# The end of the output projection, the second norm and the first MLP products under a list scheduler

## The chip, the cores and the metric

The kernel runs on one NeuronCore of a Trainium2 chip. Its engines work in parallel, each through its own queue in order: TensorE (PE; PEld is its weight load), VectorE (DVE), ScalarE (ACT), GpSimd (POOL) and SyncE (SP), which issues most DMA transfers. The metric is device time in microseconds (us), the median of several runs. A profiled execution is one run of its own, and times inside it are counted from the start of its span.

## The reference

One layer of an encoder: 1024 tokens, model width 1024.

```
h = rmsnorm(x, norm_mix_w);  proj = h @ w_in        # z, xBC, dt, q, k, v
y_ssm = ssd_mixer(...)                              # (1024, 1024)
y_na  = neighbourhood_attention(q, k, v, ...)       # 16 heads of 64
x = x + concatenate([y_ssm, y_na], axis=-1) @ w_out # w_out: 2048 x 1024
h = rmsnorm(x, norm_mlp_w)
out = x + square(relu(h @ w_mlp_in)) @ w_mlp_out    # d_ff = 4096
```

All of it is float32. The kernel splits each factor into a high part (float32r) and a low part, the rest, and forms each product from three matmuls: high by high, high by low, low by high (`mm3`, L361, and `chain`, L1217).

## The kernel before

Four phases follow each other: projection and scan; attention with the first three quarters of the w_out product beside it; the last quarter, the second norm and the first MLP product; the second MLP product.

**The planner.** The work of the scan and of the attention phase is not emitted in program order. It is entered as tasks in a `Plan` (L85), each with its engine, a cost in us, the buffers it reads and writes, and a due time for some. `order` (L141) carries due times back from each task to those it depends on. Then it takes, again and again, the task that could start first by the costs (rounded to 0.35 us), and among equals the one with the earlier due. `ready` (L182) gives the start: engine free, inputs done plus a margin (0.9 us for PE, 0.25 for the others), and a buffer of the ring free; `rings` says how many there are of each kind. `follow` (L135) takes over the free times of the plan before, and buffers entered as given count as ready at once. `run` (L1203) emits the tasks in that order and pins it on each engine (`in_order`, L1186). Instructions outside a plan are ordered by the framework (L1912 opens it with `schedule_with_timeline_sim=True`); it may move them ahead of others on their engine.

**Attention (L1249 to L1512).** Heads are worked in eight pairs. `attend` (L1351) computes scores on PE, shifts and exponents on DVE and ACT, transposes and splits the weights, and multiplies by v on PE. The result of a pair is copied from PSUM into a tile yT by ACT (L1388) and completed by DVE (L1389). `divide` (L1457) divides it on POOL (L1478), with the denominators turned and spread through DRAM on SP, and pair by pair it is stored to `na_dr` on SP ("nast"). The ring of yT holds two tiles. The planner's due for the store is 36 us after the pair's last scores.

**Last quarter of w_out (L1588 to L1607).** w_out has 2048 rows; a quarter is 512 rows. The quarters 0 to 2 are tasks of the attention plan. The weights of the last one for output columns 0 to 511 are loaded and split in that plan as well (`out_weights`, L490; L1511), without a due time; they use the ring of three split weights that the third quarter's also use. Then, outside any plan, the loop over the eight token tiles runs: for each of two column halves four steps of three matmuls into a PSUM tile "po" from a ring "mm" of two banks; an add to x2 on DVE (L1597); the store of the sum to `x2_dr` (L1598); its square sum on ACT (L1601), the root on POOL (L390, L391), the scaling on DVE in place (L1603).

**Factors and first products (L1565 to L1630, L1737 to L1749).** The MLP products use Strassen's scheme: seven products of half matrices. The left factors are seven sums and differences of quarters of the normalized x2, turned: `factors` (L1572) turns factors 1, 2 and 3 and forms the differences in place on DVE (L1585), `t_factor` (L1625) turns 6, 5, 7 and 4. Each of the 28 turned groups is four PE transposes into a PSUM tile (rings "tp" and "s", two banks each), a copy on ACT (L372) and a subtraction on DVE (L373). Products 1 and 2 of weight block 0 and product 1 of block 1 are placed among them (L1737 to L1749). Two of the three use split weights in side tiles that lie in the space of factor 4.

**The rest.** The loop over eight weight blocks (L1753) issues the other products, and the last phase the second MLP product.

Of the kernel before, what the change touches and what calls it, by code (L numbers as in the profile page):

```python
# [10 lines left out]
F32 = mybir.dt.float32  # L11
F32R = mybir.dt.float32r
# [218 lines left out]
def hymba_block(  # L231
# [258 lines left out]
    def out_weights(plan, part_, h, k2, due=None):  # L490

        Buf, task = plan.buf, plan.task
        raw, w = Buf("raw"), Buf("w")
        r0 = 512 * part_ + 256 * k2

        def load():
            raw.t = wp.tile([P, 1024], F32, tag="wraw", name="wraw", bufs=2)
            nc.sync.dma_start(
                raw.t.rearrange("p (a f) -> p a f", a=2),
                w_out[0][r0 : r0 + 256, 512 * h : 512 * h + 512].rearrange("(a p) f -> p a f", p=P),  # L500
            )

        def high():
            w.t = [wp.tile([P, 1024], F32R, tag=t, name=t, bufs=3) for t in ("wh", "wl")]
            nc.scalar.activation(w.t[0], raw.t, AF.Copy)

        def low():
            nc.gpsimd.tensor_tensor(w.t[1], raw.t, w.t[0].bitcast(F32), op=sub)
# [733 lines left out]
    with ExitStack() as ph:  # L1242
# [21 lines left out]
        for pool_, tag, n, shape, d in (  # L1264
            (cb, "nam", 1, [P, 7 * P], F32),
            (cb, "braw", 1, [P, 384], F32),
            (cb, "mb", 2, [P, 7 * P], F32),
            (ap, "pth", 1, [P, NT, 3, P], F32R),
            (ap, "ptl", 1, [P, NT, 3, P], F32R),
            (ap, "nmx", 2, [P, 8], F32),  # L1270
            (ap, "pr", 4, [P, 384], F32),
            (ap, "den", 2, [P, 2, 8], F32),
            (yt, "yT", 2, [P, T], F32),
            (ap, "rd", 1, [16, P], F32),
            (ap, "rb", 1, [P, T], F32),
        ):
            make[tag] = partial(pool_.tile, shape, d, tag=tag, name=tag, bufs=n)
# [179 lines left out]
        def divide(p, yT, yparts, den, at):  # L1457
# [43 lines left out]
        for p in range(8):  # L1501
# [13 lines left out]
        def get0(k):  # L1515
            hi, lo = get0_w[k // 2].t
            s = slice((k % 2) * 512, (k % 2) * 512 + 512)
            return hi[:, s], lo[:, s]
# [10 lines left out]
        wq, hA = (  # L1529
            b0s.enter_context(tc.tile_pool(name=n, bufs=1, side="right", reuse_waits="tile"))  # L1530
            for n in ("wq", "hA")
        )
        hc = {}

        def hc_tile(i, n):
            if i in (5, 6):
                tag = {(6, 0): "q", (6, 1): "k", (5, 0): "v", (5, 1): "kl"}[i, n]
                return b0.tile([P, 4, 512], F32R, tag=tag, name=f"h{i}", bufs=1)
            return hA.tile([P, 4, 512], F32R, tag=f"h{i}{n}", name=f"h{i}")

        def side_pair(i, n):
            t = hA.tile([P, 2, 1024], F32R, tag=f"h{i}{n}", name="wside")
            return t[:, 0], t[:, 1]

        for i in (1, 2, 3):
            hc[i] = [hc_tile(i, n) for n in range(2)]
        np_ = ph.enter_context(tc.tile_pool(name="np", bufs=2, reuse_waits="tile"))
        wb = np_.tile([P, D], F32, name="wb2", bufs=1)
        nc.sync.dma_start(wb, norm_mlp_w.partition_broadcast(P)[:, 0, :])
        h1 = []  # L1550
        for k2 in range(2):
            raw = wp.tile([P, 1024], F32, tag="wraw", name="wraw", bufs=2)
            r0 = 1536 + 256 * k2
            nc.sync.dma_start(
                raw.rearrange("p (a f) -> p a f", a=2),
                w_out[0][r0 : r0 + 256, 512:1024].rearrange("(a p) f -> p a f", p=P),
            )
            h1.append(side_pair(7, k2))
            split_to(h1[k2], raw, (nc.gpsimd, nc.vector)[k2])

        def get1(k):
            s = slice((k % 2) * 512, (k % 2) * 512 + 512)
            return h1[k // 2][0][:, s], h1[k // 2][1][:, s]

        def turned(src, i, t, tag):  # L1565
            pt = tag("ptn")
            for j in range(4):
                nc.tensor.transpose(pt[:, j * P : (j + 1) * P], src[:, j * P : (j + 1) * P], ident)
            s = (slice(None), slice(None), slice(t * P, t * P + P))
            split_from_psum(hc[i][0][s], hc[i][1][s], pt.rearrange("p (j t) -> p j t", j=4))  # L1570

        def factors(t):  # L1572
            if t < 4:
                turned(x2[:, t, 0:512], 1, t, ps_tp)
                turned(x2[:, t, 512:1024], 2, t, ps_s)
                return
            u, v = x2[:, t - 4, :], x2[:, t, :]
            turned(v[:, 512:1024], 3, t - 4, ps_tp)
            for o, p, q in (
                (u[:, 0:512], v[:, 0:512], u[:, 0:512]),  # L1580
                (v[:, 0:512], v[:, 512:1024], v[:, 0:512]),
                (v[:, 512:1024], v[:, 512:1024], u[:, 0:512]),
                (u[:, 512:1024], u[:, 512:1024], v[:, 512:1024]),
            ):
                nc.vector.tensor_tensor(o, p, q, op=sub)  # L1585

        before = None
        for t in range(NT):  # L1588
            xt = x2[:, t, :]
            for h, get in enumerate((get0, get1)):  # L1590
                pt = ps_mm("po")
                s = slice(t * P, (t + 1) * P)
                for k in range(4):
                    yh, yl = last[k]
                    mm3(pt, yh[:, s], yl[:, s], *get(k), k == 0, k == 3)
                d = xt[:, h * 512 : (h + 1) * 512]
                nc.vector.tensor_tensor(d, d, pt, op=add)  # L1597
            nc.sync.dma_start(x2_dr[t], xt)  # L1598
            jk = np_.tile([P, D], BF16, tag="jk", name="jk", bufs=1)
            ss = np_.tile([P, 1], F32, tag="ss", name="ss")  # L1600
            nc.scalar.activation(jk, xt, AF.Square, accum_out=ss)  # L1601
            r = inv_rms(np_, ss, D, 1, "r0")
            nc.vector.scalar_tensor_tensor(xt, xt, r, wb, op0=mul, op1=mul)  # L1603
            if before is not None:
                factors(before)
            before = t

    raws, hls = [wp] * 2 + [wq] * 6, [wp] * 3

# [8 lines left out]
    with ExitStack() as ph:  # L1618
# [3 lines left out]
        phase["mm"] = 4  # L1622
        hq = None

        def t_factor(i):  # L1625
            hc[i] = [hc_tile(i, n) for n in range(2)]
            for t in range(4):
                u, v = x2[:, t, :], x2[:, t + 4, :]
                src = {6: v[:, 512:1024], 5: u[:, 0:512], 7: v[:, 0:512], 4: u[:, 512:1024]}[i]
                turned(src, i, t, ps_s)  # L1630

        class Block:


            def __init__(self, fb):
                self.fb = fb
                self.a = {}
                self.load("11")
                self.X = [ps_mm("px1") for _ in range(2)]
                self.w = {}  # L1640

            def load(self, *names):
                for n in names:
# [272 lines left out]
```

## Time and profile before

| | |
|---|---|
| median of 3 runs | 1607.6 us (1606.81 to 1608.2) |
| the profiled execution | 1602.66 us |
| its span | 1600.9 us, 20796 instructions |
| DVE, ACT, POOL busy | 63%, 45%, 45% of the span |
| granted TensorE clock, mean | 0.992 |
| DMA | 278.73 MB, mean 174 GB/s |

Busy columns name the share of time in which an engine had work; PEclk is the clock granted to TensorE, as a share of its full speed. A busy TensorE at a lower clock does less. A row of waits names who waited for whom, the sum in us, how often and the longest. In the timeline a row has start, duration, engine, line, operation, output and input, and in brackets the idle time before it with what ended it. Matmuls are pipelined, and their ends are modelled: they overlap the next start.

### The profile page before, as it was taken

How to read it: one execution, taken by the hardware profiler on the slowest of the kernel's cores; microseconds unless marked ns; L12 is line 12 of the kernel's file. 1: busy time of each engine (PE TensorE's matmuls, PEld its weight loads, DVE VectorE, ACT ScalarE, POOL GpSimd, SP SyncE). 2: the span in 40 equal slices, each digit the busy share in tenths (PEclk: the TensorE clock that was granted, in tenths of full speed). 3: DMA queues.
4: the chain of work that ended last, by engine and by line, in shares of the span. 5: the costliest groups of instructions: out<-in, count | busy, mean ns of one | idle time of the engine just before them, and what ended most of it. 6: DMA issues, size and time to landing. Idle time of an engine off the chain costs nothing. (4 is left out here: it accounts for less than half of the span.)

```text
span 1600.9 us, 20796 instructions
## 1 busy us (share of the span) xinstructions
PE 1560.6 (97%) x7462; PEld 1290.7 (81%) x7462; DVE 1016.3 (63%) x1420; ACT 722.1 (45%) x1187; POOL 717.1 (45%) x524
## 2 busy tenths in 40 slices
PE   7999999999999999999999998999999989999999
PEld 5788888888878888888888776888888777888887
DVE  3776454787688845667776574544444488877763
ACT  5444333444344435657676234544444434333330
POOL 2000066774789823242364331444444465565551
PEclk9999999999999999999999999999999989999999
DMA  8212497777778786988773411444443685444232
GB/s 222 55 40 69 98 315 262 221 237 252 221 218 226 223 251 178 248 228 237 196 200 119 145 66 53 171 145 151 152 145 140 223 305 196 174 158 144 94 105 79
DMA packets 184226, 278.73 MB, mean 174 GB/s; under 512 B 14819, under 2 KB 106043, under 8 KB 184123
## 3 DMA queue, kind: packets, MB, share of 16 engines
q1 hardware_dynamic: 133323, 233.88, 48.3%
q10 hardware_dynamic: 49792, 39.85, 7.6%
q0 software_dynamic: 1008, 3.67, 0.6%
q8 instruction: 59, 0.97, 0.2%
q14 instruction: 44, 0.36, 0.1%
HBM read 191.51 MB, written 89.18 MB: 175 GB/s over the span
## 5 line engine op out<-in xcount | busy, mean ns | idle before, releaser
L368 POOL TENSOR_TENSOR wl<-wraw,wh 128x1024 fp32r<-128x1024 f32 x114 | 309.5, 2726 | 331.2 <-ACT wh L367 320.6
L367 ACT ACTIVATE wh<-wraw 128x1024 fp32r<-128x1024 f32 x126 | 132.2, 1054 | 174.7 <-PE px L1219 51.6
L362 PE MATMUL pq<-wh,hTh 128*128 128x512 f32 x512 | 204.6, 400 | 2.2 <-DVE qn L929 1.7
L363 PE MATMUL pq<-wl,hTh 128*128 128x512 f32 x512 | 200.1, 391 | 0.2 <-DVE wl L882 0.2
L364 PE MATMUL pq<-wh,hTl 128*128 128x512 f32 x512 | 200.1, 391 | 0.0
L1219 PE MATMUL px<-wh,ahl 128*128 128x512 f32 x512 | 162.6, 395 | 3.3 <-ACT ahl L367 3.3
L1219 PE MATMUL px<-h,wh 128*128 128x512 f32 x496 | 155.7, 394 | 1.4 <-DVE x L1597 1.4
L368 DVE TENSOR_TENSOR ahl<-ar,ahl 128x1024 fp32r<-128x1024 f32 x56 | 115.3, 2065 | 25.3 <-ACT ahl L367 24.2
L367 ACT ACTIVATE ahl<-ar 128x1024 fp32r<-128x1024 f32 x56 | 58.3, 1051 | 141.5 <-PE px L1219 75.0
L1219 PEld LDWEIGHTS px<-wh,ahl 128*128 128x128 f32 x512 | 97.2, 190 | 25.0 <-ACT ahl L367 3.7
L362 PEld LDWEIGHTS pq<-wh,hTh 128*128 128x128 f32 x512 | 96.3, 188 | 22.2 <-DVE qn L929 2.1
L364 PEld LDWEIGHTS pq<-wh,hTl 128*128 128x128 f32 x512 | 96.1, 188 | 20.6
L1219 PEld LDWEIGHTS px<-h,wh 128*128 128x128 f32 x496 | 92.7, 187 | 24.5 <-ACT h L372 1.6
L363 PEld LDWEIGHTS pq<-wl,hTh 128*128 128x128 f32 x512 | 96.3, 188 | 19.4 <-DVE wl L882 0.7
L1219 PE MATMUL px<-wl,ahl 128*128 128x512 f32 x256 | 101.1, 395 | 0.0
L1219 PE MATMUL px<-h,wl 128*128 128x512 f32 x248 | 97.7, 394 | 0.0
L1335 POOL TENSOR_TENSOR mb<-braw,nam 128x256 f32<-128x256 f32 (+1 forms) x48 | 38.6, 831 | 106.0 <-DVE nmx L1404 81.8
L1416 ACT ACTIVATE pr<-pr,nmx 128x384 f32<-128x384 f32 (+1 forms) x128 | 74.6, 584 | 19.6 <-DVE nmx L1404 19.0
L1219 PE MATMUL pz<-h,wh 128*128 128x512 f32 x256 | 81.7, 399 | 0.8 <-DVE h L373 0.8
L1438 DVE TENSOR_TENSOR ptl<-ptp,pth 128x384 fp32r<-128x384 f32 (+1 forms) x128 | 65.5, 521 | 26.0 <-ACT pth L1440 24.9
L1219 PE MATMUL pz<-wh,ahl 128*128 128x512 f32 x256 | 80.7, 391 | 0.8 <-DVE ahl L368 0.8
L362 PE MATMUL po<-wh,yh 128*128 128x512 f32 x192 | 80.6, 420 | 0.0
(324 smaller groups left out, 3777.5 us busy)
## 6 DMA issues: line engine op xcount, KB each, us to landing
ar<-act_dr SPq DMA_DIRECT2D x56, 512.0 KB, 3.9
act_dr<-cq SPq DMA_DIRECT2D x49, 512.0 KB, 3.2
wraw<-in_w_in_dram SPq DMA_DIRECT2D x44, 512.0 KB, 7.3
rb<-cum_dr SPq DMA_DIRECT2D x32, 512.0 KB, 6.5
wraw<-in_w_mlp_in_dram SPq DMA_DIRECT2D x32, 512.0 KB, 4.9
wraw<-in_w_mlp_out_dram SPq DMA_DIRECT2D x32, 512.0 KB, 4.7
q_dr<-hl ACTq DMA_DIRECT2D x16, 512.0 KB, 5.0
k_dr<-hl ACTq DMA_DIRECT2D x16, 512.0 KB, 3.6
```

Of the source, the lines that this page charges most:

```text
L362: nc.tensor.matmul(pt, lhsT=ah, rhs=bh, start=first, stop=False)
L363: nc.tensor.matmul(pt, lhsT=ah, rhs=bl, start=False, stop=False)
L364: return nc.tensor.matmul(pt, lhsT=al, rhs=bh, start=False, stop=last)
L367: nc.scalar.activation(hl[0], src, AF.Copy)
L368: eng.tensor_tensor(hl[1], src, hl[0].bitcast(F32), op=sub)
L1219: nc.tensor.matmul(pt, lhsT=a, rhs=b, start=f, stop=l, skip_group_check=True)
L1335: nc.gpsimd.tensor_tensor(mb.t[:, s].rearrange("p (s r c) -> p s r c", r=16, c=8), view()[:, a:b], nam.t[:, s].rearrange("p (s r c) -> p s ...
L1416: nc.scalar.activation(pr.t[:, 0:n], pr.t[:, 0:n], AF.Exp, bias=nmx.t[:, b : b + 1], scale=-1.0, accum_out=den.t[:, hh, b : b + 1],)
L1438: nc.vector.tensor_tensor(lo[0], pv3, hi.bitcast(F32), op=sub)
```

## The change

Three things change.

The ring of yT gets a third tile, and the due time of the store to `na_dr` moves from 36 to 24 us.

The weights of the last quarter for the first column half get due times (280 and 281).

The code outside the plans from L1514 to L1607 and L1737 to L1749 is replaced by a third plan. Its PSUM ring "mm" has four banks. The sixteen po groups run in a new order of token tiles; the first three are all of the first column half. Tiles 5, 6 and 7 are normalized into buffers "xn" of their own, the others in place. The four differences per pair of tiles stay; for the first three pairs two of them go to POOL. The split weights of the three first products use the ring of three, and no side tiles in the space of factor 4; the side tiles of the second half's weights (in the space of factor 7) stay. Products and transposes have due times, in us from the start of the plan. The rest of the kernel is untouched.

```diff
-            | {"nmx": 2, "pr": 4, "den": 2, "yT": 2, "rd": 1, "rb": 1}
+            | {"nmx": 2, "pr": 4, "den": 2, "yT": 3, "rd": 1, "rb": 1}
...
-            (yt, "yT", 2, [P, T], F32),
+            (yt, "yT", 3, [P, T], F32),
...
-                sp(512, lambda: na_dr[p], lambda: yT.t, reads=[yT], writes=[NA[p]], name="nast", due=at + 36)
+                sp(512, lambda: na_dr[p], lambda: yT.t, reads=[yT], writes=[NA[p]], name="nast", due=at + 24)
...
-        get0_w = [out_weights(plan, 3, 0, k2) for k2 in range(2)]
+        get0_w = [out_weights(plan, 3, 0, k2, 280.0 + k2) for k2 in range(2)]
...
-        k0 = Block(0)
-        k0.split(1)
-        k0.split(2, side_pair(4, 0))
-        k0.product(1)
-        factors(7)
-        k0.load("12", "21", "22")
-        t_factor(6)
-        k0.product(2)
-        k1 = Block(1)
-        k1.split(1, side_pair(4, 1))
-        t_factor(5)
-        t_factor(7)
-        k1.product(1)
-        t_factor(4)
+        before = plan
+        plan = Plan(
+            {"mm": 4, "tp": 2, "s": 2, "w": 3, "raw": 2, "wq": 6, "jk": 1, "ss": 2, "r0": 2, "xn": 3}
+            | {f"h{i}{n}": 1 for i in (1, 2, 3, 4, 7) for n in range(2)}
+            | {t: 1 for t in ("q0", "k0", "v0", "kl0")}
+        )
...
+        Y3 = [plan.given(Buf(tag)) for tag in ("q0", "k0", "v0", "kl0")]
+        w0 = [plan.given(Buf("w"), b.t) for b in get0_w]
...
+        XB = [Buf("xn") if t > 4 else None for t in range(NT)]
...
+        def block_product(kb, i, raw, tag, due):
+            w = split_task(raw, Buf("w"), "POOL")
...
+                    task("PE", 0.682, products, reads=[w, H[i, 0], H[i, 1]], writes=[pt], due=due + 2.75 * j + 0.69 * k, name=f"k{kb.fb}{i}")
...
+        def turned(x, h, i, t, tag, due):
...
+            task("PE", 0.44, turn, reads=[XN[x][h]], writes=[pt], due=due, name="ptn")
+            task("ACT", 0.69, lambda: nc.scalar.activation(H[i, 0].t[s], view(), AF.Copy), reads=[pt], writes=[HP[i, 0, t]], name="hi")
...
+        groups = [(0, 0), (1, 0), (2, 0), (0, 1), (1, 1), (2, 1), (4, 0), (4, 1)]
+        groups += [(3, 0), (3, 1), (5, 0), (5, 1), (6, 0), (6, 1), (7, 0), (7, 1)]
+        for m, (t, h) in enumerate(groups):
+            pt, d, at = Buf("mm"), x2[:, t, halves_[h]], 3.2 * m
...
+                task("PE", 0.682, products, reads=[Y3[k], (w0, w1)[h][k // 2]], writes=[pt], due=at + 0.7 * k, name="po")
...
+            load(512, partial(lambda t: x2_dr[t], t), partial(lambda xt: xt, xt), reads=X2[t], due=at + 12, name="x2st")
...
+            if t < 4:
+                turned(t, 0, 1, t, "tp", at + 13)
+                turned(t, 1, 2, t, "s", at + 14)
+                continue
+            u = t - 4
+            turned(t, 1, 3, u, "tp" if u < 3 else "s", at + 13)
+            difference("DVE", (u, 0), (t, 0), (u, 0))
+            difference("POOL" if u < 3 else "DVE", (t, 0), (t, 1), (t, 0))
+            difference("DVE", (t, 1), (t, 1), (u, 0))
+            difference("POOL" if u < 3 else "DVE", (u, 1), (u, 1), (t, 1))
+            late = 58 + 1.5 * u if u < 3 else at + 14
+            turned(u, 1, 4, u, "tp" if u < 3 else "s", at + 15)
+            turned(t, 1, 6, u, "s", late)
+            turned(u, 0, 5, u, "tp" if u < 1 else "s", late + 0.5)
+            turned(t, 0, 7, u, "s", late + 1)
+        k0, k1 = Block(0), Block(1)
...
+        wk1, X = block_product(k0, 1, raw0["11"], "mm", 49.5)
+        wk2, Y = block_product(k0, 2, raw0["12"], "tp", 61.0)
...
+        wk3, Z = block_product(k1, 1, block_load(k1, "11"), "mm", 56.0)
+        plan.follow(before)
+        run(plan, make)
```

More of the change, by code (lines that the diff above doesn't have):

```diff
@@ L1525, in hymba_block @@
         pa.close()
[L1529 to L1606, printed above, removed]
+    wq, hA = (
+        b0s.enter_context(tc.tile_pool(name=n, bufs=1, side="right", reuse_waits="tile"))
+        for n in ("wq", "hA")
+    )
@@ L1608, in hymba_block, with hc_tile @@
+    hc = {}
+    def hc_tile(i, n):
+        if i in (5, 6):
+            tag = {(6, 0): "q", (6, 1): "k", (5, 0): "v", (5, 1): "kl"}[i, n]
+            return b0.tile([P, 4, 512], F32R, tag=tag, name=f"h{i}", bufs=1)
+        return hA.tile([P, 4, 512], F32R, tag=f"h{i}{n}", name=f"h{i}")
     raws, hls = [wp] * 2 + [wq] * 6, [wp] * 3
@@ L1636, in __init__ @@
                 self.fb = fb
[L1637 to L1640, printed above, removed]
+                self.a, self.w = {}, {}
+                if fb > 1:
+                    self.load("11")
+                    self.X = [ps_mm("px1") for _ in range(2)]
             def load(self, *names):
@@ new lines, in hymba_block @@
+        wb = np_.tile([P, D], F32, name="wb2", bufs=1)
+        before = plan
[3 more added lines that the diff above has]
+            | {t: 1 for t in ("q0", "k0", "v0", "kl0")}
+        )
+        Buf, part, task = plan.buf, plan.part, plan.task
+        load = partial(load_task, plan)
+        make = {
+            "mm": lambda: ps_mm("po"),
+            "tp": lambda: ps_tp("ptn"),
+            "s": lambda: ps_s("ptn"),
+            "raw": lambda: wp.tile([P, 1024], F32, tag="wraw", name="wraw", bufs=2),
+            "wq": lambda: wq.tile([P, 1024], F32, tag="wraw", name="wraw", bufs=6),
+            "w": lambda: [wp.tile([P, 1024], F32R, tag=t, name=t, bufs=3) for t in ("wh", "wl")],
+            "jk": lambda: np_.tile([P, D], BF16, tag="jk", name="jk", bufs=1),
+            "ss": lambda: np_.tile([P, 1], F32, tag="ss", name="ss"),
+            "r0": lambda: np_.tile([P, 1], F32, tag="r0", name="r0"),
+            "xn": lambda: np_.tile([P, D], F32, tag="xn", name="xn", bufs=3),
+        }
@@ new lines, in hymba_block, with split_task @@
+        HP = {(i, n, t): part(H[i, n]) for i, n in H for t in range(4)}
+        load(512, lambda: wb, lambda: norm_mlp_w.partition_broadcast(P)[:, 0, :], writes=[WB], due=0.0, name="wb")
+        def split_task(src, w, lo, due=None):
+            task("ACT", 1.06, lambda: nc.scalar.activation(w.t[0], src.t, AF.Copy), reads=[src], writes=[w], name="wh")
+            eng, cost = (nc.gpsimd, 2.42) if lo == "POOL" else (nc.vector, 1.23)
+            task(lo, cost, lambda: eng.tensor_tensor(w.t[1], src.t, w.t[0].bitcast(F32), op=sub), reads=[src], writes=[w], due=due, name="wl")
+            return w
@@ new lines, in side_tile @@
+        def side_tile(k2):
+            t = hA.tile([P, 2, 1024], F32R, tag=f"h7{k2}", name="wside")
+            return t[:, 0], t[:, 1]
+        w1 = []
+        for k2 in range(2):
+            raw, w = Buf("raw"), Buf(f"h7{k2}")
+            w.maker = partial(side_tile, k2)
+            r0 = 1536 + 256 * k2
+            load(
+                512,
+                partial(lambda raw: raw.t.rearrange("p (a f) -> p a f", a=2), raw),
+                partial(lambda r0: w_out[0][r0 : r0 + 256, 512:1024].rearrange("(a p) f -> p a f", p=P), r0),
+                writes=[raw],
+                name="raw",
+            )
+            w1.append(split_task(raw, w, ("POOL", "DVE")[k2]))
@@ new lines, in normed, with turn @@
+        def normed(t, h):
+            whole = XB[t].t if XB[t] else x2[:, t, :]
+            return whole[:, 512 * h : 512 * h + 512]
+        def turned(x, h, i, t, tag, due):
+            pt = Buf(tag)
+            s = (slice(None), slice(None), slice(t * P, t * P + P))
+            def turn():
+                for j in range(4):
+                    nc.tensor.transpose(pt.t[:, j * P : (j + 1) * P], normed(x, h)[:, j * P : (j + 1) * P], ident)
+            view = lambda: pt.t.rearrange("p (j t) -> p j t", j=4)
+            task("PE", 0.44, turn, reads=[XN[x][h]], writes=[pt], due=due, name="ptn")
+            task("ACT", 0.69, lambda: nc.scalar.activation(H[i, 0].t[s], view(), AF.Copy), reads=[pt], writes=[HP[i, 0, t]], name="hi")
+            task("DVE", 0.73, lambda: nc.vector.tensor_tensor(H[i, 1].t[s], view(), H[i, 0].t[s].bitcast(F32), op=sub), reads=[pt, HP[i, 0, t]], writes=[HP[i, 1, t]], due=due + 3, name="lo")
@@ new lines, in hymba_block, with products, root @@
+        for m, (t, h) in enumerate(groups):
+            pt, d, at = Buf("mm"), x2[:, t, halves_[h]], 3.2 * m
+            for k in range(4):
+                def products(pt=pt, k=k, h=h, t=t):
+                    yh, yl = last[k]
+                    hi, lo = (w0, w1)[h][k // 2].t
+                    f, s = slice((k % 2) * 512, (k % 2) * 512 + 512), slice(t * P, (t + 1) * P)
+                    mm3(pt.t, yh[:, s], yl[:, s], hi[:, f], lo[:, f], k == 0, k == 3)
+                task("PE", 0.682, products, reads=[Y3[k], (w0, w1)[h][k // 2]], writes=[pt], due=at + 0.7 * k, name="po")
+            task("DVE", 0.69, partial(lambda d, pt: nc.vector.tensor_tensor(d, d, pt.t, op=add), d, pt), reads=[pt], writes=[X2[t][h]], due=at + 4.5, name="x2")
+            if not h:
+                continue
+            xt = x2[:, t, :]
+            load(512, partial(lambda t: x2_dr[t], t), partial(lambda xt: xt, xt), reads=X2[t], due=at + 12, name="x2st")
+            jk, ss, r0 = Buf("jk"), Buf("ss"), Buf("r0")
+            task("ACT", 1.3, partial(lambda xt, jk, ss: nc.scalar.activation(jk.t, xt, AF.Square, accum_out=ss.t), xt, jk, ss), reads=X2[t], writes=[jk, ss], name="sq")
+            def root(ss=ss, r0=r0):
+                nc.gpsimd.tensor_scalar(r0.t, ss.t, 1.0 / D, EPS, op0=mul, op1=add)
+                nc.gpsimd.tensor_tensor(r0.t, r0.t, half[:, 0:1], op=ALU.pow)
+            task("POOL", 0.8, root, reads=[ss], writes=[r0], name="r0")
+            task("DVE", 1.4, partial(lambda t, xt, r0: nc.vector.scalar_tensor_tensor(XB[t].t if XB[t] else xt, xt, r0.t, wb, op0=mul, op1=mul), t, xt, r0), reads=[r0, WB, *X2[t]], writes=XN[t], name="norm")
+            if t < 4:
+                turned(t, 0, 1, t, "tp", at + 13)
+                turned(t, 1, 2, t, "s", at + 14)
+                continue
+            u = t - 4
[9 more added lines that the diff above has]
+            turned(t, 0, 7, u, "s", late + 1)
@@ L1751, in hymba_block @@
+        for i in (1, 2, 3, 6, 5, 7, 4):
+            hc[i] = [H[i, n].t for n in range(2)]
+        nps.close()
         x2s.close()
```

49 lines of the change are left out of this document (39 added, 10 removed).

## The prediction

> **What bounds the kernel now.** I read the page first, its busy shares and its forty slices.
>
> ```profile
> PE 1560.6 (97%) x7462; PEld 1290.7 (81%) x7462; DVE 1016.3 (63%) x1420; ACT 722.1 (45%) x1187; POOL 717.1 (45%) x524
> PE   7999999999999999999999998999999989999999
> ```
>
> TensorE is the bound nearly everywhere, and the change leaves its matmuls as they are. So the change is worth the time that TensorE loses in the stretches it reorders, and no more. Those are the attention phase and the stage after it, up to the first MLP products, at about 610 to 983 us. I asked the windows for TensorE time and granted clock there; these are the windows that stand out (the columns are named in the first line).
>
> ```profile
> core 0: us, PE busy (x) PEld busy (x) DVE busy (x) ACT busy (x) POOL busy (x), PEclk, DMA share, GB/s
> 700.00:705.00 5.00, 2.13 (x8) 1.67 (x8) 2.75 (x7) 3.00 (x8) 0.00 (x0) 0.76 0.95 320
> 705.00:710.00 5.00, 5.00 (x18) 4.24 (x17) 2.80 (x8) 1.47 (x5) 0.00 (x0) 0.56 0.41 129
> 890.40:983.00 92.60, 82.92 (x391) 65.54 (x390) 62.40 (x76) 36.08 (x56) 27.50 (x24) 0.96 0.26 91
> 906.40:911.40 5.00, 5.00 (x15) 3.96 (x16) 0.89 (x2) 3.05 (x5) 3.50 (x5) 0.66 0.87 283
> 966.00:978.40 12.40, 7.92 (x51) 5.16 (x49) 7.47 (x12) 7.23 (x13) 0.00 (x0) 1.00 0.00 1
> 978.40:983.00 4.60, 4.54 (x13) 3.62 (x14) 1.86 (x4) 3.03 (x4) 0.00 (x0) 0.63 0.00 0
> ```
>
> Two kinds of loss show: waits, and a lowered clock just behind them. A full busy column with PEclk 0.56 is still lost time. The clock rows give 5 x 0.24 + 5 x 0.44 = 3.4 us lost at 700 to 710, 5 x 0.34 = 1.7 at 906, and 4.6 x 0.37 = 1.7 at 978. Next I took the waits from the waits view. Around 700 us ACT waits for a store to land, and TensorE behind it; the only other wait of TensorE in the attention phase of over one us is for a load (us in total, times, longest).
>
> ```profile
> ACT yT L1388 <- DMA na_dr<-yT: 5.0, 1, 5.0
> ...
> PE pv L1368 <- DMA q<-q_dr: 1.2, 1, 1.2
> ```
>
> A matmul's modelled end overlaps the next, so I cost the waits by start times in the timeline of TensorE (start, duration).
>
> ```profile
> 699.76 0.40 PE L364 MATMUL po<-wh,yl 128*128 128x512 f32 x1
> 703.02 0.55 PE L1368 MATMUL pv<-pth,v 128*128 128x256 f32 x1 [2.87 <-DVE yT L1389]
> ...
> 892.12 0.40 PE L362 MATMUL po<-wside,q 128*128 128x512 f32 x1
> 892.93 0.50 PE L363 MATMUL po<-wl,v 128*128 128x512 f32 x1 [0.41 <-POOL wl L508]
> ...
> 893.97 0.40 PE L364 MATMUL po<-wh,kl 128*128 128x512 f32 x1
> 895.14 0.51 PE L362 MATMUL po<-wh,q 128*128 128x512 f32 x1 [0.78 <-DVE x L1597]
> ...
> 903.24 0.40 PE L363 MATMUL po<-wside,kl 128*128 128x512 f32 x1
> 903.47 0.40 PE L364 MATMUL po<-wside,kl 128*128 128x512 f32 x1
> 906.33 0.50 PE L362 MATMUL po<-wh,q 128*128 128x512 f32 x1 [2.46 <-DVE x L1597]
> ...
> 945.87 0.60 PE L1568 MATMUL ptn<-ident,x 128*128 128x128 f32 x4
> 947.85 0.70 PE L1219 MATMUL px<-h,wh 128*128 128x512 f32 x2 [1.38 <-DVE x L1597]
> ...
> 954.45 0.60 PE L1568 MATMUL ptn<-ident,x 128*128 128x128 f32 x4
> 954.81 1.64 PE L1219 MATMUL px<-h,wside 128*128 128x512 f32 x6
> ...
> 966.10 0.60 PE L1568 MATMUL ptn<-ident,x 128*128 128x128 f32 x4
> ...
> 968.11 1.33 PE L1568 MATMUL ptn<-ident,x 128*128 128x128 f32 x8 [0.74 <-DVE h L373]
> ...
> 978.46 0.50 PE L1219 MATMUL pz<-h,wh 128*128 128x512 f32 x1 [0.75 <-DVE h L373]
> ```
>
> A 512-wide matmul follows the last at 0.23 us (903.24 to 903.47) and a group of four transposes takes 0.36 (954.45 to 954.81). Losses by start to start, less that work: at 700, 3.26 - 0.23 = 3.0. In the stage, 0.6 at 892, 0.9 at 894, 2.6 at 903, 1.6 at 946, and from 966.10 to 978.46 12.4 us that hold twelve groups (the rows left out are like that at 968.11) of transposes and one matmul, 4.6 us of work, so 7.7. With the two clock terms of the stage, 1.7 each, the stage loses 16.8 us; the stall at 700 with its clock loses 6.4. Together 23.2 us can be won.
>
> **The third y tile.** With two tiles, the copy of pair 2's result into yT (ACT, L1388) waits until pair 0's store to na_dr has landed; behind it in ACT's queue stand the exponents and splits of the attention, and TensorE waits for those. With three, pair 2 takes a fresh tile, and pair 3 reuses pair 0's some thirty us later, long after that landing. The wait goes, and with it the 3.0 us and, if the clock follows the gap, the 3.4. What is late next? By the row above the next late thing is one of 1.2 us, which no clock drop follows, so I count the gain in full. Moving the store's due time 12 us forward makes the divide and its small transfers come sooner; each is an instruction already there, so this costs nothing unless it blocks SP's queue (a rival below).
>
> The clock drops sit directly behind the gaps of 3.0 and 2.6 us and behind the transposes with 0.75 us gaps, so I take the clock back with them. The Trainium skill, "TensorE: Matmul & The Clock Gate", section "What's actually happening", ties the drop to an idle window of about 3.4 us; the rows here drop after less, and by its rule read to the letter these terms would stay. That is a rival below.
>
> **The last quarter of w_out.** The first stall (892) stays. The second weight tile of the first half is split by POOL only when the last weights of the quarter before are free, and its low half is what the row at 892.93 waits for. The planner treats these weights as given, so it starts the first group of products straight through. I leave 0.8 us of loss there: from 892.1, when the matmul that needs only the high half has gone, to 892.93. A due time of 280 doesn't change which buffer is free. The next two stalls (894, 903) are TensorE waiting for a PSUM bank: only two "mm" banks, and the evacuating add queues behind other VectorE work. These are the rows of VectorE (groups, then one instruction of its timeline), ACT and POOL in the stage:
>
> ```profile
> L373 DVE TENSOR_TENSOR h<-ptn,h 128x512 fp32r<-128x512 f32 x28 | 18.7, 687 | 9.3 <-ACT h L372 9.3
> L1597 DVE TENSOR_TENSOR x<-x,po 128x512 f32<-128x512 f32 x16 | 10.8, 683 | 15.5 <-PE po L364 15.5
> L1603 DVE SCALAR_TENSOR_TENSOR x<-x,r,wb 128x1024 f32<-128x1024 f32 x8 | 10.2, 1280 | 1.7 <-DMA x_dr<-x 1.4 <-POOL r L391 0.4
> ```
>
> ```profile
> 902.28 3.40 DVE L1664 TENSOR_TENSOR wraw<-wraw 128x1024 f32<-128x1024 f32 x1
> ```
>
> ```profile
> L372 ACT ACTIVATE h<-ptn 128x512 fp32r<-128x512 f32 x28 | 16.0, 596 | 19.1 <-PE ptn L1568 18.7
> L1601 ACT ACTIVATE jk<-x 128x1024 bf16<-128x1024 f32 x8 | 8.4, 1054 | 20.3 <-DVE x L1597 20.3
> ```
>
> ```profile
> L391 POOL TENSOR_TENSOR r<-r,half 128x1 f32<-128x1 f32 x8 | 4.8, 599 | 0.6
> L390 POOL TENSOR_SCALAR r<-ss 128x1 f32<-128x1 f32 x8 | 2.6, 326 | 25.1 <-ACT jk L1601 24.9
> ```
>
> The add that frees the bank TensorE takes at 906.33 stood behind the 3.4 us of L1664, which ended at 905.7. With four banks a group of twelve matmuls (12 x 0.23 = 2.75 us) may be evacuated three groups, about 8 us, late before TensorE notices; no row of VectorE comes near that. Starting with three token tiles of the first half also puts 3 x 2.75 = 8.3 us ahead of the second half's weights. So 0.9, 2.6 and the clock's 1.7 go.
>
> **Norm, factors and products.** The stall at 946 (first MLP product waiting for a bank) goes with the four banks. The 7.7 us are the large term: twelve groups of transposes in a row, each waiting for its PSUM tile to be copied (ACT 0.6, L372) and subtracted (VectorE 0.69, L373), with nothing between them because the three products had all been issued earlier. In the changed order the products come due at 49.5 to 66 and the late transposes at 58 to 63, so they interleave. A pair of groups takes 2.07 us alone (966.10 to 978.46 divided by six), or 1.03 a group. Behind the last w_out product there are some 14 late groups: 14.5 us at that pace. The cover is the three products, 72 matmuls x 0.23 = 16.8 us, plus 14 x 0.36 = 5 us of their own TensorE time. It suffices, but the two later products are 11.2 us, and the planner spends the first one before most of these become due; its order assumes longer evacuations than the trace has, so some three to five groups may stand at the end without cover at 0.6 us each. I leave 3 us of loss there, between 0 and the old 7.7.
>
> The last token tile's chain is the other thing that could be late: add 0.7 (L1597), square 1.1 (L1601), root 0.9 (L390 and L391), scale 1.3 (L1603), four differences at 0.7 (L1585, below), then five groups of transposes at 1.03. That is about 12 us, against the same 22 us of cover. It does not decide.
>
> Six differences move from VectorE to POOL. POOL does a 128x512 in-SBUF operation in 1.3 us, and VectorE slows when both run:
>
> ```profile
> L1478 POOL TENSOR_TENSOR yT<-yT,rb x16: 1287/1297/1323, 689.3 to 878.2; 128x512 f32<-128x512 f32 x16
> ...
> L1585 DVE TENSOR_TENSOR x<-x x16: 674/684/2878, 933.2 to 960.4; 128x512 f32<-128x512 f32 x16
> ```
>
> One difference took 2.88 us instead of 0.68, and L1664 above 3.4. If each of the six costs VectorE its whole 1.3 us, that is 7.8 us more in a queue that is busy 62.4 of 92.6 us; there is room, so I price it at nothing on TensorE. If it falls into the last chain it adds at most 2.2 us, still inside the cover. The Trainium skill, "SBUF — State Buffer", section "Who interferes with whom", says VectorE with two SBUF inputs is shut out for the whole POOL instruction; the 2.88 agrees, and by it the sum stays as it is.
>
> The loads of MLP weights and the x2 stores stay the same in number, and DMA is at 0.26 in the stage. Normalized tiles 5 to 7 go to buffers of their own, so they don't wait for their store; the wait so saved (1.4 us, L1603) was VectorE's. For other waits that a new order of the whole attention phase brings I put in 1 us, between -2 and 4.
>
> **The sum.** 23.2 - 0.8 - 3 - 1 = 18.4 us. The profiled execution took 1602.66 us (span 1600.9 and 1.8 around it) and would take 1584.3. It lies 4.9 us under the median of 1607.6; I take the difference off the median: 1589.2 us.
>
> **The rivals.** First, the transposes remain paced by their evacuation, because the planner's order leaves them together. Then 7.7 and the clock's 1.7 stay and only 23.2 - 9.4 - 0.8 - 1 = 12 us are won: 1595.6. For it speaks that the pace is fixed by two PSUM banks; against it the due times. Second, another wait replaces the one at 700, so that only the stage gains: 18.4 - 6.4 = 12, 1595.6 as well. Third, the clock does not come back with the gaps, or drops elsewhere: 18.4 - 6.8 = 11.6, 1596.0. Against it speaks that each drop in these stretches has a gap ahead of it. By the Trainium skill's rule named above this would be the outcome. Fourth, the hand-made order is not better than the one the framework found: 1607. Against it: the gaps are in the trace and the banks are doubled.
>
> Slower: SP's queue is in order, and the store of each pair's result waits for POOL's divide at its head.
>
> ```profile
> SPq L395 <- POOL yT L1478: 9.8, 5, 4.6
> ```
>
> ```profile
> DVE pr L1404 <- POOL mb L1335: 3.0, 2, 1.9
> ```
>
> Moved 12 us forward, it may stand ahead of the bias loads, which VectorE already just misses twice. If at four of the seven pair changes the bias comes late by as much as yT did, each costs 3.0 + 3.4 = 6.4 us: 25.6 against the 18.4, 7 slower, 1614.8. From three on it decides. Against it: five such waits are there now, and none reaches TensorE.
>
> **How the numbers follow.** Forecast 0.60, transposes 0.12, replaced wait 0.10, clock 0.06, no gain 0.05, slower 0.07. A change of 0.2%, 3.2 us, is about what a measurement of this kernel can tell. Faster: 0.60 + 0.12 + 0.10 + 0.06 = 0.88; same 0.05; slower 0.07. The range goes from all of the 23.2 and one us more, 1583, to the three middle rivals with the 4 us bound of other waits on top, 1600. Left out are the last two cases.
>
> **What would show it.** Right: no wait of ACT for na_dr, PEclk 1.00 over 700 to 710; "mm" waits of po gone; PEclk 1.00 through the stage; the transposes interleaved with px and py, the stage some 12 us shorter. A row of eight or more transposes with 0.75 us before each would show the first rival; a new gap over 2 us in 610 to 890, the second; TensorE waiting for mb or psc, the slower one. A gain under 8 us makes the prediction wrong.

## The result, and the profile after

| | us |
|---|---|
| before, median of 4 runs | 1607.2 (1606.04 to 1608.2) |
| after, median of 4 runs | 1590.93 (1589.17 to 1593.62) |
| ratio | 0.990 (95%: 0.9883 to 0.9918) |
| after again, later, medians of 6 runs and of 11 of before | 1593.32 against 1605.34, ratio 0.9924 (0.9904 to 0.9944) |
| profiled execution of after | 1591.7, span 1589.9 |

The change is worth 16.3 us by the first comparison and 12.0 by the second. The profiled executions differ by less, 1602.66 - 1591.7 = 11.0 us; that of before lies 4.5 us under its median. What follows accounts for these 11.0. Three single runs of the later batches, 7144.65 and 5699.14 us of before and 1719.17 of `e10_x_early`, lie far outside all others, and the ratios leave them out.

The page of after has TensorE's 7462 matmuls as before, in 5.4 us less:

```profile
PE 1555.2 (98%) x7462; PEld 1288.3 (81%) x7462; DVE 1009.7 (64%) x1414; ACT 722.8 (45%) x1187; POOL 730.6 (46%) x530
```

The windows of after (the last row but two is the whole stage, from the first matmul of the last quarter to the first store of an activated product; the same two marks stand at 890.5 and 982.5 in before):

```profile
core 0: us, PE busy (x) PEld busy (x) DVE busy (x) ACT busy (x) POOL busy (x), PEclk, DMA share, GB/s
640.00:645.00 5.00, 4.12 (x27) 3.55 (x25) 0.92 (x4) 1.20 (x3) 0.00 (x0) 1.00 1.07 257
645.00:650.00 5.00, 3.61 (x13) 3.03 (x14) 3.99 (x12) 3.13 (x9) 2.39 (x3) 0.71 1.08 231
700.00:705.00 5.00, 5.00 (x32) 4.57 (x31) 3.77 (x10) 3.54 (x10) 1.28 (x2) 1.00 1.08 338
705.00:710.00 5.00, 5.00 (x34) 4.51 (x33) 2.92 (x10) 3.62 (x11) 0.00 (x0) 1.00 1.05 199
885.30:971.40 86.10, 80.20 (x386) 64.84 (x386) 59.04 (x70) 35.66 (x56) 39.45 (x30) 0.96 0.36 123
951.00:956.00 5.00, 4.93 (x23) 4.07 (x23) 4.12 (x8) 2.62 (x5) 0.00 (x0) 0.67 0.18 62
968.30:971.70 3.40, 3.40 (x10) 2.71 (x9) 1.49 (x3) 2.56 (x3) 0.00 (x0) 0.55 0.52 151
```

700 to 710 is now full at full clock. But the stage still has a clock of 0.96, as before: it took 92.0 us and takes 86.1, 5.9 less, where the forecast had some 12. A new low clock stands at 645. The longest waits of TensorE in these two phases are these (two more take 0.5 and 0.4):

```profile
PE ptn L1756 <- POOL x L1768: 2.5, 1, 2.5
PE pv L1368 <- DMA q<-q_dr: 2.3, 1, 2.3
PE ptn L1756 <- DVE h L1761: 1.6, 2, 1.3
PE po L363 <- POOL wl L508: 0.7, 1, 0.7
PE px L1219 <- ACT cq L1626: 0.6, 1, 0.6
```

ACT's wait for the store to na_dr is gone, and so are the two po waits for a bank. What is left can be costed by start times, as before, in TensorE's timeline:

```profile
643.90 0.22 PE L1368 MATMUL pv<-pth,v 128*128 128x128 f32 x1
646.39 0.33 PE L1368 MATMUL pv<-ptl,v 128*128 128x128 f32 x1 [2.27 <-DMA q<-q_dr]
...
886.72 0.40 PE L362 MATMUL po<-wh,v 128*128 128x512 f32 x1
887.82 0.50 PE L363 MATMUL po<-wl,v 128*128 128x512 f32 x1 [0.70 <-POOL wl L508]
...
947.57 0.60 PE L1756 MATMUL ptn<-ident,xn 128*128 128x128 f32 x4
950.66 2.99 PE L1756 MATMUL ptn<-ident,x 128*128 128x128 f32 x12 [2.50 <-POOL x L1768]
953.30 1.16 PE L1219 MATMUL px<-h,wh 128*128 128x512 f32 x2
...
964.08 0.60 PE L1756 MATMUL ptn<-ident,x 128*128 128x128 f32 x4
965.98 0.66 PE L1756 MATMUL ptn<-ident,x 128*128 128x128 f32 x4 [1.30 <-DVE h L1761]
966.58 0.66 PE L1756 MATMUL ptn<-ident,xn 128*128 128x128 f32 x4
967.80 1.12 PE L1219 MATMUL px<-h,wh 128*128 128x512 f32 x2 [0.57 <-ACT cq L1626]
```

Start to start, less 0.23 for a matmul and 0.36 for four transposes: 0.9 at 887, 2.7 at 948, and from 964.08 to 967.80 3.7 - 1.1 = 2.6. Two short waits at 943 and 961 add about 1. The clock loses 5 x 0.33 = 1.7 behind the gap at 948 and 3.4 x 0.45 = 1.5 behind the last one. Together 10.4 us stay in the stage. Before lost 16.8, and 16.8 - 10.4 = 6.4 is about the 5.9 by which the stage is shorter. In the attention phase 2.3 us and 5 x 0.29 = 1.5 are lost at 644, where before had 1.2; the 6.4 at 700 are gone. That phase (first po matmul to the mark of the stage) fell from 271.9 to 267.6, 4.3 us. The rest of the program makes up 0.8. So the question is why the stage gave half of what was forecast.

What stood before the gap at 948 is seen on VectorE and on POOL:

```profile
946.40 2.86 DVE L1768 TENSOR_TENSOR xn<-xn,x 128x512 f32<-128x512 f32 x1
```

```profile
945.36 3.35 POOL L368 TENSOR_TENSOR wl<-wraw,wh 128x1024 fp32r<-128x1024 f32 x1
949.34 1.27 POOL L1768 TENSOR_TENSOR x<-x,xn 128x512 f32<-128x512 f32 x1 [0.63 <-DVE xn L1768]
```

A difference on VectorE takes 2.86 us, and ends half a microsecond after a split on POOL that belongs to a later weight; only then the fourth difference of that pair runs on POOL, for which TensorE waits. The pair is that of token tiles 2 and 6, the third of four. The split (L368) is not a task of the third plan: it comes from the loop over weight blocks, and the framework put it between the plan's instructions on POOL. I had two theories. **A**: the two engines shut each other out, so that moving differences to POOL, which I had priced at nothing, is what costs. **B**: the order pinned on TensorE puts these transposes too early for the chain of differences, whatever engine makes them, since the planner's costs and due times are not the chip's.

### The profile page after: what moved, and what is told of

Same layout as the page of the kernel before. It is cut to its first block, busy times and chain, and to the rows that moved or that the text cites. A ratio compares the mean times of both kernels' runs of the same rounds, so it can differ in the third digit from the quotient of the medians.

```text
span 1589.9 us, 20811 instructions
## 1 busy us (share of the span) xinstructions
PE 1555.2 (98%) x7462; PEld 1288.3 (81%) x7462; DVE 1009.7 (64%) x1414; ACT 722.8 (45%) x1187; POOL 730.6 (46%) x530
## 5 line engine op out<-in xcount | busy, mean ns | idle before, releaser
L368 POOL TENSOR_TENSOR wl<-wraw,wh 128x1024 fp32r<-128x1024 f32 x113 | 308.2, 2739 | 309.1 <-ACT wh L367 281.0
L1219 PE MATMUL px<-h,wh 128*128 128x512 f32 x512 | 162.9, 399 | 0.6 <-ACT cq L1626 0.6
L368 DVE TENSOR_TENSOR ahl<-ar,ahl 128x1024 fp32r<-128x1024 f32 x56 | 115.3, 2065 | 22.8 <-ACT ahl L367 21.7
L1219 PEld LDWEIGHTS px<-h,wh 128*128 128x128 f32 x512 | 96.2, 189 | 24.1 <-ACT cq L1626 0.8
L1219 PE MATMUL px<-h,wl 128*128 128x512 f32 x256 | 101.4, 396 | 0.0
L1404 DVE CUSTOM_DVE_ANT_0 pr<-psc,mb 128x384 f32<-128x384 f32 (+1 forms) x128 | 64.8, 520 | 28.7 <-PE psc L1401 21.1
L1438 DVE TENSOR_TENSOR ptl<-ptp,pth 128x384 fp32r<-128x384 f32 (+1 forms) x128 | 65.5, 521 | 23.2 <-ACT pth L1440 22.3
```

Of the source, the lines that this page charges most:

```text
L368: eng.tensor_tensor(hl[1], src, hl[0].bitcast(F32), op=sub)
L1219: nc.tensor.matmul(pt, lhsT=a, rhs=b, start=f, stop=l, skip_group_check=True)
L1404: nc.vector.tensor_tensor_reduce(pr.t[:, 0:n], pt.t[:, 0:n], mb.t[:, o : o + n], scale=-1.0, scalar=3.0e38, op0=add, op1=ALU.min, accum_ou ...
L1438: nc.vector.tensor_tensor(lo[0], pv3, hi.bitcast(F32), op=sub)
```

## The experiments

### The two parts alone

`e1_yt_only` is before with the first part only, `e2_stage_only` is after without it.

```
- yT ring 2, nast due=at + 36
+ yT ring 3, nast due=at + 24        # e1; e2 the other way round
```

> The kernel before with the third yT tile and the store's due of 24 alone. Theory (the parts add up, the wait for the store to na_dr costs 3.0 us and its clock 3.4, and a longer wait for the q loads near 645 us takes some of it back): 4 to 6 us under the kernel before, no wait of ACT for na_dr near 700 us, the stage from 890 us as before. Rival (the third tile only shifts the wait to other places, and the whole gain lies in the stage): within 1.5 us of the kernel before.

> The changed kernel with two yT tiles and the store's due of 36. Theory (the parts add up): 10 to 12 us under the kernel before, the stall near 700 us there again, the stage as in the changed kernel. Rival (the gain lies in the stage alone): 16 us under the kernel before, as much as the whole change.

`e1_yt_only`: median 1597.16 against 1603.83, ratio 0.9959 (0.9944 to 0.9973), 6.7 us. `e2_stage_only`: 1596.51, ratio 0.9960 (0.9944 to 0.9975), 7.3 us by the medians and 6.4 by the ratio, less than the 10 to 12 that I had expected of it. The parts add up to 13 or 14, which lies between the two measurements of the change. In e2 the old stall is back:

```profile
PE pv L1368 <- DVE yT L1389: 4.0, 1, 4.0
...
PE ptn L1756 <- POOL x L1768: 2.4, 1, 2.4
```

So the third tile, with the earlier store, gave about what was forecast for it, 6.4 (its interval goes from 4.3 to 9.0), and the stage about half.

### Theory A: the two engines

`e3_diff_dve` makes all differences on VectorE; `e5_both_dve` also makes the splits of the three first products there. Neither moves the splits of the later weights (L368), which stay on POOL.

```
- difference("POOL" if u < 3 else "DVE", ...)    # twice
+ difference("DVE", ...)
- w = split_task(raw, Buf("w"), "POOL")          # e5 only
+ w = split_task(raw, Buf("w"), "DVE")
```

> The changed kernel with all sixteen differences on VectorE, none on POOL. Theory (the 2.7 us wait of TensorE near 948 us for a difference on POOL, with the clock drop behind it, comes from VectorE and POOL shutting each other out: VectorE's 2.86 us difference ended with POOL's split, and POOL's own difference came after it): 3 to 5 us under the changed kernel, the wait gone. Rival (the planner places the transposes of the last two pairs before their tiles can be ready, whichever engine does the differences): within 1.5 us of the changed kernel, the same wait with VectorE as releaser.

> The changed kernel with all differences and also the low halves of the three first products' weights on VectorE, so that POOL does only one split of the w_out weights and the roots in the stage. Theory (exclusion of VectorE by POOL): the differences take 0.68 us each, 3 to 5 us under the changed kernel, at least as fast as with the differences alone moved. Rival (VectorE is too full: it gets some 11 us more work): slower than the changed kernel by 2 us or more, TensorE waiting for VectorE's subtractions behind the transposes.

Ratios 0.9930 (0.9908 to 0.9953) and 0.9925 (0.9904 to 0.9947), the same as after's 0.9924 in its second comparison. The waits of TensorE, first of e3, then of e5:

```profile
PE ptn L1756 <- DVE x L1768: 2.5, 2, 1.9
...
PE ptn L1756 <- DVE h L1761: 2.0, 3, 0.9
```

```profile
PE ptn L1756 <- DVE h L1761: 3.3, 4, 1.4
PE ptn L1756 <- DVE x L1768: 1.7, 1, 1.7
```

The same chain is waited for, under VectorE's name instead of POOL's, and neither kernel brought the 3 to 5 us that I had expected. So the place of these six differences is worth nothing that can be measured, and theory A falls as far as it blames them. But the exclusion itself was not taken away: POOL's split of the later weight stands beside the third difference of tiles 2 and 6 in these kernels too. In e5 (VectorE, POOL, TensorE):

```profile
942.66 2.88 DVE L1768 TENSOR_TENSOR xn<-xn,x 128x512 f32<-128x512 f32 x1
```

```profile
941.97 3.01 POOL L368 TENSOR_TENSOR wl<-wraw,wh 128x1024 fp32r<-128x1024 f32 x1
```

```profile
946.41 0.63 PE L1756 MATMUL ptn<-ident,x 128*128 128x128 f32 x4 [1.71 <-DVE x L1768]
```

Alone that difference takes 0.69. Were it 2.2 us shorter, the wait of 1.71 would be covered, by an estimate from these rows in which nothing else moves; in e3 (2.68 and a wait of 1.86) it comes out the same. No run moves L368 off POOL, so this form of theory A is untested.

### Theory B: the planner's order

`e6_after` is after itself, for comparison on the same chip. `e7_late` gives earlier due times to the late transposes, so that they stand less bunched behind the last products. `e9_margin` lowers the margin by which the planner thinks TensorE's inputs come late, from 0.9 to 0.3 us. `e8_best` is e5 with e7's due times, and the first three groups' products with the second weight tile put 6 us later in the plan.

```
- late = 58 + 1.5 * u if u < 3 else at + 14
+ late = 49 + 1.0 * u if u < 3 else at + 6           # e7, e8
+ plan.MARGIN = plan.MARGIN | {"PE": 0.3}            # e9
+ po: due=at + 0.7 * k + (6.0 if m < 3 and k > 1 else 0.0)   # e8
```

> The changed kernel itself, beside the others on one chip. Theory (the gains of the two parts, 0.41% and 0.40% in their own runs, add up): 12 to 14 us under the kernel before. Rival (the two parts help each other, since the first run of the change showed 16 us): 16 us or more under the kernel before.

> The changed kernel with earlier due times for the late transposes (factors 6, 5 and 7): 49 + u for the first three pairs instead of 58 + 1.5 u, and 8 us earlier for the last pair, so that they stand among all three products. Theory (the transposes at the end are bare because the first product is spent before they become due, and their evacuation sets the pace): the six bare groups at the end, 3.2 us of waits and the clock drop behind them, shrink to two or three; 2 to 5 us under the changed kernel. Rival (the differences and norms are not ready any earlier, so the transposes only stall earlier): within 1.5 us of the changed kernel, with the waits at about 945 us.

> The changed kernel with the earlier due times for the late transposes, all differences and the low halves of the three products' weights on VectorE, and the third and fourth steps of the first three po groups due 6 us later, so that their first steps cover the wait for the second weight tile. Theory (exclusion, bare transposes and the weight tile are three separate costs): 4 to 8 us under the changed kernel; the wait of 0.7 us for POOL at the start of the stage gone. Rival (VectorE becomes the bound): no faster than the kernel with earlier due times alone.

> The changed kernel with the planner's margin for TensorE at 0.3 us instead of 0.9 in the third plan, so that it assumes a quicker evacuation and places transposes closer together. Theory (the planner's slow model of evacuation is why groups stay over for the end): fewer bare groups at the end, 1 to 4 us under the changed kernel. Rival (the margin keeps TensorE from waiting): the same number of groups moved, but waits of 0.3 to 1 us before many of them, as slow as the changed kernel or up to 3 us slower.

Against before's 1605.34: e6 1593.32, ratio 0.9924 (0.9904 to 0.9944); e7 1588.12, 0.9904 (0.9881 to 0.9927); e9 1587.68, 0.9899 (0.9871 to 0.9927); e8 1591.84, 0.9918 (0.9894 to 0.9943). e9 has the lowest median of all, and it and e7 lie 5 to 6 us under e6, a little more than I had expected of either; but the intervals overlap, so a gain over after is likely and not shown. e8, from which I had expected the most, lies only 1.5 under e6. In e7 the wait for POOL's difference is gone and another of its size stands instead; in e9 no wait of the transposes is longer than 1.6 (e7, then e9):

```profile
PE ptn L1756 <- DVE h L1761: 3.7, 2, 3.0
```

```profile
PE ptn L1756 <- DVE h L1761: 2.7, 3, 1.6
...
PE ptn L1756 <- POOL x L1768: 1.7, 2, 1.2
```

For theory B this is support: only due times or a margin differ, and the waits move with the order. It isn't proof against the rest of theory A. Ahead of e7's gap of 3.0, which ends at 954.09, VectorE's subtraction stands behind a difference that the same split on POOL holds up (VectorE, then POOL); e9 has such a difference of 2.75 us as well:

```profile
949.96 2.74 DVE L1768 TENSOR_TENSOR x<-xn,x 128x512 f32<-128x512 f32 x1
```

```profile
948.80 3.35 POOL L368 TENSOR_TENSOR wl<-wraw,wh 128x1024 fp32r<-128x1024 f32 x1
```

In e8 the wait for the second weight tile stayed at 0.7, so these later due times did not cover it.

A pair of gaps is worth a look. These are the windows of e6 and of e7 around the longest gap of the stage, which is 2.49 us at 952.8 in e6 and 2.99 us at 954.1 in e7:

```profile
950.00:955.00 5.00, 1.73 (x14) 1.25 (x13) 4.97 (x6) 1.68 (x3) 2.13 (x2) 1.00 0.37 105
955.00:960.00 5.00, 5.00 (x31) 4.24 (x29) 3.62 (x6) 3.09 (x5) 1.78 (x1) 1.00 0.00 0
```

```profile
950.00:955.00 5.00, 2.01 (x11) 1.43 (x10) 4.97 (x5) 0.22 (x1) 2.15 (x1) 1.00 0.31 85
955.00:960.00 5.00, 5.00 (x32) 4.05 (x32) 3.73 (x7) 3.49 (x6) 0.78 (x1) 1.00 0.06 20
```

The clock stays at 1.00 behind both, while the same gap of 2.50 in after's profile (the same kernel as e6) was followed by 0.67. Behind the last gap of the stage the clock drops in both: at 968 in after, and at 969 in e6 (0.74 over 970 to 975).

### The order of token tiles, and the buffers of their own

`e12_natural` keeps the planner and the four banks and takes the tiles in their old order, both column halves of each. `e13_in_place` normalizes all tiles in place.

```
- groups = [(0, 0), (1, 0), (2, 0), (0, 1), (1, 1), ...]
+ groups = [(t, h) for t in range(NT) for h in range(2)]   # e12
- XB = [Buf("xn") if t > 4 else None for t in range(NT)]
+ XB = [None for t in range(NT)]                           # e13
```

> The changed kernel with the po groups in the order of token tiles 0 to 7, both column halves of a tile in turn, as in the kernel before. Theory (the new order hides the wait for the second half's weights and starts the differences earlier): 2 to 5 us over the changed kernel, TensorE waiting some 2 us or more for the side weights in the second group. Rival (the planner hides this wait itself, since products of other groups are free to go first): within 1.5 us of the changed kernel.

> The changed kernel with all token tiles normalized in place, none in a buffer of its own. Theory (VectorE would wait for the store of the last tiles, and the last chain has little cover left): 1 to 4 us over the changed kernel, with VectorE waiting for the stores to x2_dr. Rival (the stores land in time): within 1.5 us of the changed kernel.

`e12_natural`: median 1602.33 against 1602.81, ratio 0.9986 (0.9965 to 1.0008): no gain is left, some 10 us less than with the new order, where I had expected 2 to 5. In its profile the attention phase keeps 3.5 us of its gain (268.4 against 271.9), and the stage loses as much. Its waits:

```profile
PE ptn L1756 <- DVE h L1761: 4.7, 4, 2.8
PE ptn L1756 <- POOL x L1768: 4.0, 2, 2.6
...
PE po L362 <- ACT wside L1695: 1.6, 1, 1.6
PE po L363 <- DVE wside L1697: 0.8, 1, 0.8
PE po L363 <- POOL wside L1697: 0.7, 1, 0.7
```

The second half's weights (wside) come late, 3.1 us together, and the transposes wait 8.7 instead of 4.5. Its stage takes 95.3 us, 3.3 more than that of before. `e13_in_place`: 1594.12, ratio 0.9945 (0.9928 to 0.9961). By its point that is 3 us over after, with an interval that overlaps after's second one, 0.9904 to 0.9944, and not its first. VectorE waits for no store in its stage, so the mechanism that I had expected isn't there; whether the separate buffers are worth 3 us or nothing stays open.

### The stall at 644

The row of TensorE above names a load of q as what ended this wait. The row of its weight load names VectorE's ptl, and VectorE's own row names a load of x:

```profile
DVE x L1326 <- DMA x<-in_x_dram: 4.1, 1, 4.1
PEld pv L1368 <- DVE ptl L1438: 2.5, 1, 2.5
```

So VectorE's add of the attention phase (L1326) waits for a load of x there, and the ptl that TensorE's next pv needs stands behind it in VectorE's queue. `e10_x_early` gives these loads a due time 8 us ahead; `e11_combo` adds e7's and e9's edits.

```
- sp(256, ..., writes=[d], name="x", since=0.5)
+ sp(256, ..., writes=[d], name="x", since=0.5, due=at - 8)
```

> The changed kernel with an earlier due time for the loads of x in the attention phase (8 us before its product instead of about 3 us after). In every profile so far, of the kernel before too, an add of VectorE near 645 us waits 2.0 to 6.9 us for such a load, with TensorE behind it for up to 5.1 us. Theory (this one wait, common to both kernels, is a good part of the spread between runs and eats part of what the third yT tile gains): the wait gone, 2 to 5 us under the changed kernel, and less spread. Rival (the DMA engines are full there, so that an earlier load of x delays another load that TensorE then waits for): within 1.5 us of the changed kernel, with a wait for q, k, v or the bias instead.

> The changed kernel with the earlier x loads, the earlier due times of the late transposes (49 + u, and 8 us earlier for the last pair) and the planner's margin of 0.3 us for TensorE in the third plan. Theory (three separate costs): 5 to 9 us under the changed kernel, 18 to 21 us under the kernel before. Rival (margin and due times cure the same wait): no more than 1 us under the better of the two kernels that had one of them, 0.990 of the kernel before.

`e10_x_early`: median 1597.25 against 1602.81, ratio 0.9957 (0.9938 to 0.9976), by its point worse than after, with intervals that overlap a little. The wait for x is gone, and its timeline shows a larger one (ACT, ACT, PE):

```profile
689.20 1.06 ACT L505 ACTIVATE wh<-wraw 128x1024 fp32r<-128x1024 f32 x1 [8.64 <-DMA wraw<-in_w_out_dram]
...
690.17 0.47 ACT L1440 ACTIVATE pth<-ptp 128x384 fp32r<-128x384 f32 x1
...
690.69 0.58 PE L1368 MATMUL pv<-pth,v 128*128 128x256 f32 x1 [6.34 <-ACT pth L1440]
```

Behind it comes a clock of 0.52 from 689.2 to 696.1. The loads of x now stand in SP's queue ahead of a load of w_out, which is issued at 679.98 instead of 674.02; ACT, in order, waits 8.6 us for it with the attention's split behind it. That load stands behind one of the bias as well, which waits 2.5 us for POOL; so its delay comes from the order of the queue. The DMA engines are nearly full there (shares of 0.75 to 1.10 in the windows from 660 to 690), and ACT gets the weights 9 us after the issue; how much of the stall is due to that isn't separated. `e11_combo` has the same stall and comes to 0.9937 (0.9915 to 0.9958), short of the 18 to 21 us under before that I had expected.

## Why the prediction was right, and where a step failed

The time lies in the range, and 1.7 us above the forecast of 1589.2. Part of that closeness is chance: the forecast took 18.4 us off, the two comparisons gave 16.3 and 12.0, and 12.0 is also what three of the rivals gave (11.6 to 12). The number alone does not tell them apart; the rows do.

**Right.** The third tile: 6.4 forecast, 6.7 measured alone, with the earlier store (in after's profile the phase gives 4.3, since 2.6 us more are lost at 644). The second weight tile's wait: 0.8 left over, 0.9 found. The two bank waits of po (0.9 and 2.6) and the clock behind them: gone, with TensorE full from 890 to 940. That the tile order puts time ahead of the second half's weights: e12 shows what happens without it. The bare transposes at the end: 3 us left, 2.6 found. SP's queue: its wait behind POOL's divide did grow, from 9.8 us to this in after, and no wait of TensorE for mb or psc followed, as the slower rival would have needed:

```profile
SPq L395 <- POOL yT L1478: 24.1, 5, 9.2
```

**The step that failed** is the pricing of the differences: "there is room, so I price it at nothing on TensorE", and at worst 2.2 us, "still inside the cover". With it goes "It does not decide" on the chain of add, square, root, scale and four differences. I set 12 us against 22 us of cover as two sums, and only for the last token tile. The chain that was late is that of the pair before, tiles 2 and 6: its third difference took 2.86 us on VectorE instead of 0.68, and its fourth stood on POOL behind a split of 3.35. The cover is not a pool that TensorE draws on when it is idle: its order is pinned by the planner's costs; the products issued by then were spent, and the next one (953.30) stood behind three groups of transposes whose chain was late. This gap, 2.7 us, with the 1.7 of clock behind it accounts for 4.4 of the 6 us or so by which the stage fell short. By e3 and e5 it makes no measurable difference which engine makes the differences; in e7 and e9 the gaps move with the order. How much of the gap the exclusion by the later weight's split makes stays open.

**The clock** is the second mis-sized term. I took all drops back because the old gaps go. Two came again in the stage, 1.7 behind the gap of 2.7 and 1.5 behind that of 1.5 and the short ones after it. The same kernel's other profile (e6) has none behind its gap of 2.49. So the rival "clock not back" held in part, and at that gap by chance of the execution; the drop behind the last gap stands in both profiles. The Trainium skill, "TensorE: Matmul & The Clock Gate", section "What's actually happening", calls the window by which the clock is set free-running, so that one kernel measures differently from run to run; the gaps of 2.50 and 2.49 in after and e6 agree. Its idle window of 3.4 us does not stand as a threshold: 2.3 us sufficed at 644 in after, and 3.0 did not in e7.

**What is late next in the attention** I answered with the 1.2 us of before's profile, "which no clock drop follows", and read it as a wait for the load of q; it is VectorE's wait for x there too (3.1 us in before). In after TensorE waits 2.3 with a drop. Eight profiles of kernels with the same attention plan show VectorE waiting for x from 2.0 us (e5) to 6.9 (e8):

```profile
DVE x L1326 <- DMA x<-in_x_dram: 2.0, 1, 2.0
```

```profile
DVE x L1326 <- DMA x<-in_x_dram: 6.9, 1, 6.9
```

So one profile's value doesn't carry over to a kernel with another third plan. Whether it also varies between executions of one kernel isn't shown: after and e6, the same kernel, both have 4.1. That it explains part of the spread of before (1593.85 to 1611.19 on one chip) is argued, not shown. The rival of a replaced wait held in part for after, whose loss at 644 grew from 1.2 to 3.8 us, and in full for e10.

Two slips in the sum are small: the stall at 892 stands in the 23.2 with 0.6 us, and I took 0.8 off for it; and 72 x 0.23 is 16.6, not 16.8.

**What stays open**: whether the gap at 948 would go if POOL's split of the later weight stood elsewhere; whether e7's and e9's orders are faster than after; and how much of 16.3 against 12.0 is more than spread, since the intervals overlap. The four banks were not run alone, nor the third tile without the earlier store.

## What to carry to other kernels

Cover counts only in the order in which it is issued: take the pinned order, and ask for each late chain, not only the last, which work stands between its end and its user, instead of comparing two sums. Look also for instructions from outside the plan that come to stand between the plan's own. Price a gap of two or three microseconds on TensorE at itself plus a chance of 1.7 us of clock or more, and read a wait for a transfer from several profiles. In a queue that is in order, a load brought forward delays those behind it, and a longer queue may stand behind one of these.

## What the hardware showed that I had not expected

Gaps of 2.3 and 2.5 us in after were followed by a lowered clock (0.71 and 0.67 in the windows behind them), one of 2.49 in e6 and one of 2.99 in e7 were not; a low stretch cost 1.5 to 1.7 us behind these gaps, and 3.3 to 3.4 behind the stalls at 700 in before and at 690 in e10. A 128x512 difference on VectorE took 2.86 us beside a POOL split of 3.35, and ended only after it, where it takes 0.68 alone. The Trainium skill, "SBUF — State Buffer", section "Who interferes with whom", calls the shared port pair an exclusive lock, and the rows agree. How much TensorE loses by it no run here separates.
